# Attention in a two-layer decoder trunk: one matmul for the scores of both kinds of keys, and the compressed branch's products stacked along the contraction

## The chip, the core and the metric

The kernel runs on one core of a Trainium2 chip. The metric is the device time of one execution in microseconds (us). Of the engines, TensorE (PE in the rows; its weight loads are PEld) does the matmuls and transposes, VectorE (DVE) and ScalarE (ACT) do the elementwise work, GpSimd (POOL) small side work, and SyncE (SP) issues the weight transfers.

## The reference, cut to what matters

Two layers; in each, a feed-forward block, a mixer with three branches, and a second feed-forward block, over 256 tokens of width 1024. The change is in the mixer's sparse attention, which has 8 heads of width 64 in 2 groups of 4 heads that share keys and values. For the 256 tokens here it computes, for each head:

```python
# compressed branch: 15 keys, one for each 32 tokens at a stride of 16
s_c = einsum('bqghd,bgnd->bghqn', qp, kc) * scale
p_c = masked_softmax(s_c, cmp_end <= t)
o_c = einsum('bghqn,bgnd->bqghd', p_c, vc)
# selected blocks (all 4 blocks of 64 tokens are taken) and sliding window (512 >= 256 tokens):
# with this length both are plain causal attention, each with keys and values of its own
s_s = einsum('bqghd,bgqld->bghql', qr, ks) * scale ; p_s = masked_softmax(s_s, m_s)
s_w = einsum('bqghd,bkgd->bghqk', qr, kw) * scale  ; p_w = masked_softmax(s_w, m_w)
return g[..., 0:1] * o_c + g[..., 1:2] * o_s + g[..., 2:3] * o_w
```

All of it is float32. The kernel keeps that precision by splitting an operand into a rounded high part and a low rest, and by adding three matmuls (high by high, high by low, low by high).

## The kernel before, in words

The 256 tokens are two tiles of 128 rows, t = 0 and t = 1. Each tile is a stream, written as a Python generator that runs through both layers; the program takes steps of the two streams in turn. A step is the matmuls of one unit of weights: 1024 columns, six matmuls of 512 columns (three for each of two pieces). The weights of a unit come by a transfer on SP's queue, are split into a high and a low part by ScalarE (`whi`, lines 272 and 276) and VectorE (`wlo`, lines 273 and 277) up to 4 steps ahead, and lie in 8 pairs of buffers.

Beside the streams runs a list of background tasks, up to four at a time (`background`, line 1063). After each step of a stream one task gets one turn, and each task names after a turn how many steps it wants to rest: `ATT_A, ATT_B, ATT_C, ATT_D = 1, 3, 2, 3`. Attention is made of such tasks. The stream of a tile waits for their result only ahead of its last branch product (`until ... S["ynsa"][t]`). The final order on each engine's queue is not quite that of the program: it is set when the kernel is built, where an instruction that is expected to be ready may pass an earlier one that is not.

For each tile and layer there are four tasks `nsa_attention(t, l, var, g)` (line 730): `var` is the kind of keys (0 selected, 1 window), `g` the group of heads. A task of the first tile sees 128 keys. It does eight matmuls of 128 columns into one PSUM bank `s` (4 heads, high and low keys, line 745), adds the causal mask, takes the maximum and the exponentials (lines 750 to 757), scales by the reciprocal sum and the gate (line 764), transposes the four blocks of probabilities (line 769), splits them into `ph` and `pl` (lines 368 and 369), and adds three matmuls of 512 columns into the tile's bank `o` (line 788). With the call that ends it, a task of the first tile takes five turns. A task of the second tile sees 256 keys: it works through two banks `s`, each with four matmuls of 256 columns, and two blocks of keys, in seven turns.

The compressed branch has one task `cmp_attention` for each tile and layer (line 895). Its probabilities are 128 tokens by 8 heads by 16 keys, `sc`, 128 columns in all; one transpose (line 918) turns them, a copy and a subtraction split them into `phc`. The values were laid out by `compress` (line 795) as `vbd`, block-diagonal by head: for each of 4 heads in a group a 128 by 128 weight, in a high and a low form (line 890). For each of the four the task does three matmuls of 128 columns, 12 in all (line 788).

PSUM has 8 banks: 6 for accumulators (`acc`, `br`, `s`, `sc`, `o` and others, in turn), 2 for transposes (`pt`). Temporaries of 520 columns have 8 buffers in turn.

Of the kernel before, what the change touches and what calls it, by code (L numbers as in the profile page):

```python
# [21 lines left out]
F32 = mybir.dt.float32  # L22
# [6 lines left out]
P = 128  # L29
# [49 lines left out]
class Nothing:  # L79
    """Stands in for engines, pools and tiles while the order of the weight units is found."""  # L80

# [13 lines left out]
def view(ap, off, dims):  # L95
    if isinstance(ap, Nothing):
        return ap
    return bass.AP(tensor=ap.tensor, offset=ap.offset + off, ap=[list(ap.ap[0])] + [list(d) for d in dims])


def f32(ap):
    return ap.bitcast(F32)
# [18 lines left out]
def program(nc, pools, a, out, plan):  # L121
# [21 lines left out]
    def tbank():  # L143
        return pst.tile([P, 512], F32, name="pt", tag="t")
# [4 lines left out]
    def ttile(name, dt=F32):  # L149
        return tp.tile([P, 520], dt, name=name, tag="tmp")  # L150

# [1 line left out]
    x = [consts.tile([P, D], F32, name=f"x{t}") for t in range(2)]  # L153
# [36 lines left out]

# [1 line left out]
    now = [0]  # L192
# [186 lines left out]

# [1 line left out]
    def rstd(halves):  # L381
# [63 lines left out]

# [1 line left out]
    def ffn(t, l, which):  # L447
# [34 lines left out]

# [1 line left out]
    dmask = consts.tile([P, P], F32, name="dmask")  # L484
    cmadd = consts.tile([P, 2, 16], F32, name="cmadd")
    cm01 = consts.tile([P, 2, 16], F32, name="cm01")
    bmask = consts.tile([P, 8], F32, name="bmask")
    cosT = consts.tile([P, 2, 8], F32, name="cosT")
    sinT = consts.tile([P, 2, 8], F32, name="sinT")
# [3 lines left out]
    def setup():  # L493
# [6 lines left out]
        for t in range(2):  # L500
            for m, fill in ((cmadd, NEG), (cm01, 0.0)):
# [6 lines left out]
        nc.gpsimd.affine_select(bmask, bmask, pattern=[[16, 8]], compare_op=OP.is_ge, fill=0.0,  # L508
                                base=15, channel_multiplier=-1)
        for t in range(2):  # L510
            nc.gpsimd.memset(f32(vz[t]), 0.0)
# [41 lines left out]

# [1 line left out]
    shared = {}  # L555
# [46 lines left out]

# [1 line left out]
    def rope(src, n, t, write):  # L604
# [117 lines left out]
    def recip_gate(sums, n, gate):  # L722
        r = sp.tile([P, n], F32, name=f"rg{n}")
        nc.vector.tensor_scalar(r, sums, 1e-30, None, op0=OP.max)
        nc.vector.reciprocal(r, r)
        if gate is not None:
            nc.vector.tensor_mul(r, r, gate)
        return r

    def nsa_attention(t, l, var, g):  # L730
        S = shared[l]
        QT = S["QT"][t][1]
        KT = [k.rearrange("p (v k) -> p v k", v=4) for k in S["KT"]]
        gt = S["gt"][t]
        nk = t + 1
        hp = 4 // nk
        sums = sp.tile([P, 4], F32, name="sums")
        pu = []
        for u in range(nk):
            s = bank("s")  # L740
            s3 = s.rearrange("p (i k) -> p i k", i=hp)
            for i in range(hp):
                lhsT = QT[:, g * 4 + u * hp + i]
                for j in range(2):
                    nc.tensor.matmul(s3[:, i], lhsT=lhsT, rhs=KT[j][:, var * 2 + g, 0:nk * P],  # L745
                                     start=(i == 0 and j == 0), stop=(i == hp - 1 and j == 1),
                                     skip_group_check=True)
            yield ATT_A
            dg = s3[:, :, t * P:(t + 1) * P]
            nc.vector.tensor_tensor(dg, dg, view(dmask, 0, [[0, hp], [1, P]]), op=OP.add)  # L750
            nm = sp.tile([P, hp], F32, name=f"nm{hp}")
            nc.vector.tensor_reduce(nm, s3, axis=AX.X, op=OP.max, negate=True)
            p = ttile("p")
            p3 = p[:, :512].rearrange("p (i k) -> p i k", i=hp)
            for i in range(hp):
                c = u * hp + i
                nc.scalar.activation(p3[:, i], s3[:, i], AF.Exp, bias=nm[:, i:i + 1], accum_out=sums[:, c:c + 1])
            pu.append(p3)
        yield ATT_B
        r = recip_gate(sums, 4, view(gt, g * 12 + 1 + var, [[3, 4]]))  # L760
        for u in range(nk):
            for i in range(hp):
                c = u * hp + i
                nc.vector.tensor_scalar(pu[u][:, i], pu[u][:, i], r[:, c:c + 1], None, op0=OP.mult)
        yield ATT_C
        for kt in range(nk):
            pt = tbank()
            for c in range(4):
                nc.tensor.transpose(pt[:, c * P:(c + 1) * P], pu[c // hp][:, c % hp, kt * P:(kt + 1) * P], ident)
            ph, pl = ttile("ph", F32R), ttile("pl", F32R)  # L770
            evac_split(ph[:, :512], pl[:, :512], pt)
            yield ATT_D
            vh = vz[kt][:, var * 512 + g * 128:var * 512 + g * 128 + 128]
            vl = vz[kt][:, var * 512 + 256 + g * 128:var * 512 + 256 + g * 128 + 128]
            accumulate(t, l, 1, [(None, st, mv[:, :512]) for st, mv in ((vh, ph), (vh, pl), (vl, ph))], kt == nk - 1)

    def accumulate(t, l, part, products, last):
        S = shared[l]
        first = S["o"][t] is None
        if first:  # L780
            S["o"][t] = bank("o")
        o = S["o"][t]
        if last:
            S["parts"][t] += 1
        closing = last and S["parts"][t] == 5
        for n, (i, st, mv) in enumerate(products):
            dst = o if i is None else o[:, i * P:(i + 1) * P]
            nc.tensor.matmul(dst, lhsT=st, rhs=mv, start=(first and (n == 0)),  # L788
                             stop=(closing and n == len(products) - 1), skip_group_check=True)
        if closing:  # L790
            y = gtile("ynsa", F32R)
            evac_split(y[:, 0:512], y[:, 512:1024], o)
            S["ynsa"][t] = y

    def compress(l, i):
# [68 lines left out]
        else:  # L864
# [4 lines left out]
            gr = ttile("gr", F32R)  # L869
            out_v = gr[:, 0:256].rearrange("p (a i n) -> p a i n", a=4, i=4)  # L870
            out_l = gr[:, 256:512].rearrange("p (a i n) -> p a i n", a=4, i=4)
            src = view(u1, 0, [[16, 4], [0, 4], [1, 16]])
            nc.scalar.copy(out_v, src)
# [3 lines left out]
            for ht in range(2):  # L877
                mm3(ps[:, 0:64], gr[:, ht * P:(ht + 1) * P], gr[:, 256 + ht * P:256 + (ht + 1) * P],
                    wh[:, ht], wl[:, ht], ht == 0, ht == 1)
            vs = sp.tile([P, 64], F32, name="vs")  # L880
            nc.scalar.copy(vs, ps[:, 0:64])
            vbd = gtile("vbd", F32R)
            vf = sp.tile([P, 64], F32R, name="vf")
            nc.scalar.copy(vf, vs)
            vlo = sp.tile([P, 64], F32, name="vlo")
            nc.vector.tensor_sub(vlo, vs, f32(vf))
            msk = view(bmask, 0, [[1, 4], [4, 2], [0, 64]])
            for j, sv in enumerate((f32(vf), vlo)):
                dst = vbd[:, j * 512:(j + 1) * 512].rearrange("p (i g d) -> p i g d", i=4, g=2)
                nc.vector.tensor_tensor(dst, view(sv, 0, [[0, 4], [0, 2], [1, 64]]), msk, op=OP.mult)  # L890
            S["VBD"] = vbd
            for tt in range(2):
                add(("nsa", l, tt), cmp_attention(tt, l))

    def cmp_attention(t, l):
# [18 lines left out]
        r = recip_gate(sm, 8, view(S["gt"][t], 0, [[3, 8]]))  # L914
        nc.vector.tensor_tensor(sc, sc, view(r, 0, [[1, 8], [0, 16]]), op=OP.mult)
        yield ATT_B
        pt = tbank()
        nc.tensor.transpose(pt[:, :P], sc.rearrange("p h n -> p (h n)"), ident)
        ph = ttile("phc", F32R)
        evac_split(ph[:, 0:P], ph[:, P:2 * P], pt[:, :P])  # L920
        yield ATT_D
        vbd = S["VBD"]
        products = []
        for i in range(4):
            vh, vl = vbd[:, i * P:(i + 1) * P], vbd[:, 512 + i * P:512 + (i + 1) * P]
            products += [(i, st, mv) for st, mv in ((vh, ph[:, 0:P]), (vh, ph[:, P:2 * P]), (vl, ph[:, 0:P]))]
        accumulate(t, l, 0, products, True)

# [122 lines left out]

# [1 line left out]
    pending, lanes, counts = [], [], {}  # L1053
# [26 lines left out]
    def mixer(t, l):  # L1080
# [21 lines left out]
        def attend():  # L1102
            for var in range(2):
                for g in range(2):
                    add(("nsa", l, t), nsa_attention(t, l, var, g))

# [109 lines left out]
```

## Time and profile before

| what | value |
|---|---|
| median of 3 timed runs | 1317.28 us (1317.2 to 1317.69) |
| the profiled execution: span from first to last instruction | 1314.1 us |
| its own time, with what lies around the span | not on the page; the median is 3.2 us above the span |
| instructions | 17407 |
| TensorE matmuls | 6266, busy 1300.3 us |
| VectorE, ScalarE, GpSimd busy | 896.6 us, 743.0 us, 76.5 us |
| transfers | 240.76 MB, mean 183 GB/s |
| mean granted TensorE clock | 0.999 |

Matmuls are pipelined: the record of one lasts longer than the time until the next one starts. What a matmul takes from the engine is read from the distance of two starts, not from its own length.

### The profile page before, as it was taken

To read this page: it belongs to the slowest core of one execution; us is meant where nothing else is said; L and a number is where in the kernel's file an instruction comes from. 1 tells how busy PE (TensorE), PEld (TensorE's weight loads), DVE (VectorE), ACT (ScalarE), POOL (GpSimd) and SP (SyncE) were. 2 spreads that over 40 slices of the span, in tenths; PEclk is the share of its full clock that TensorE was granted. 3 is DMA by queue.
4 is the path that set the end of the run, shared out by engine and by line. 5 is a ranking of instruction groups with operands and counts; after the bars stand their busy time and mean duration, and the time that the engine had idled before them with its cause. 6 is when DMAs were issued, how large, how long until landed. Compare 5 with 4: busy or idle time off the path is not lost.

```text
span 1314.1 us, 17407 instructions
## 1 busy us (share of the span) xinstructions
PE 1300.3 (99%) x6266; PEld 1078.9 (82%) x6266; DVE 896.6 (68%) x1363; ACT 743.0 (57%) x1195; POOL 76.5 (6%) x184
## 2 busy tenths in 40 slices
PE   9999999999999999999999999999999999999998
PEld 7888888878888888888888888888888888888886
DVE  6666556989887666565575665579898866766643
ACT  6645546886664465454464555568666554645542
POOL 3010101200000010000010001013000000100000
PEclk9999999999999999999999999999999999999999
DMA  8665575764445655655756665657644456566552
GB/s 273 210 192 181 180 220 175 224 214 144 139 134 159 198 187 180 191 192 180 229 168 191 188 209 177 209 167 230 191 144 145 133 159 210 176 188 189 183 190 80
DMA packets 118950, 240.76 MB, mean 183 GB/s; under 512 B 8176, under 2 KB 26768, under 8 KB 118864
## 3 DMA queue, kind: packets, MB, share of 16 engines
q1 hardware_dynamic: 118256, 239.30, 58.0%
q8 instruction: 49, 0.80, 0.2%
q0 software_dynamic: 576, 0.34, 0.1%
q14 instruction: 37, 0.30, 0.1%
q10 hardware_dynamic: 32, 0.01, 0.0%
HBM read 238.57 MB, written 1.05 MB: 182 GB/s over the span
## 4 chain that ended last, share of the span: by engine, by line
PE 90%; DVE 4%; ACT 2%; DMA 2%; issue 1%; POOL 0%; SPq 0%; DVEq 0%; POOLq 0%; ACTq 0%
PE acc L334 19%; PE acc L336 19%; PE acc L335 19%; PE y L336 7%; PE y L335 7%; PE y L334 7%; PE pt L377 3%; PE o L788 2%; PE br L334 2%; PE br L335 2%; PE br L336 2%; DVE wlo L277 1%; DMA raw<-in_ffn_w_in_dram 1%; PE s L745 1%; ACT whi L276 1%
## 5 line engine op out<-in xcount | busy, mean ns | idle before, releaser
L277 DVE SCALAR_TENSOR_TENSOR wlo<-raw,gT,whi 128x512 fp32r<-128x512 f32 (+2 forms) x432 | 397.6, 938 | 208.0 <-ACT whi L276 206.7
L276 ACT ACTIVATE whi<-raw,gT 128x512 fp32r<-128x512 f32 (+2 forms) x432 | 365.9, 874 | 295.3 <-PE acc L336 216.6
L334 PE MATMUL acc<-whi,hThi 128*128 128x512 f32 (+1 forms) x1184 | 468.6, 396 | 1.0 <-ACT hThi L368 1.0
L336 PE MATMUL acc<-whi,hTlo 128*128 128x512 f32 (+1 forms) x1184 | 459.1, 389 | 0.0
L335 PE MATMUL acc<-wlo,hThi 128*128 128x512 f32 (+1 forms) x1184 | 458.6, 388 | 0.1
L336 PEld LDWEIGHTS acc<-whi,hTlo 128*128 128x128 f32 x1184 | 222.1, 188 | 46.9 <-DVE hTlo L369 0.6
L334 PEld LDWEIGHTS acc<-whi,hThi 128*128 128x128 f32 x1184 | 222.5, 188 | 43.1 <-ACT hThi L368 1.8
L335 PEld LDWEIGHTS acc<-wlo,hThi 128*128 128x128 f32 x1184 | 222.7, 188 | 41.8 <-DVE wlo L277 0.8
L273 DVE TENSOR_TENSOR wlo<-raw,whi 128x1024 fp32r<-128x1024 f32 x144 | 176.0, 1224 | 108.2 <-ACT whi L272 106.1
L272 ACT CAST whi<-raw 128x1024 fp32r<-128x1024 f32 x144 | 151.2, 1051 | 130.9 <-PE acc L336 70.6
L334 PE MATMUL y<-whi,gT 128*128 128x512 f32 x352 | 138.1, 392 | 0.0
L336 PE MATMUL y<-whi,gT 128*128 128x512 f32 x352 | 137.4, 390 | 0.0
L335 PE MATMUL y<-wlo,gT 128*128 128x512 f32 x352 | 137.4, 390 | 0.0
L389 POOL TENSOR_TENSOR nr<-nv,mhalf 128x1 f32<-128x1 f32 x28 | 19.9, 712 | 1017.6 <-DVE nv L387 1013.8
L336 PEld LDWEIGHTS y<-whi,gT 128*128 128x128 f32 x352 | 66.1, 188 | 13.8
L335 PEld LDWEIGHTS y<-wlo,gT 128*128 128x128 f32 x352 | 66.1, 188 | 13.3
L334 PEld LDWEIGHTS y<-whi,gT 128*128 128x128 f32 x352 | 66.1, 188 | 13.3
L368 ACT CAST gT<-pt 128x512 fp32r<-128x512 f32 (+1 forms) x48 | 26.1, 543 | 23.3 <-PE pt L377 23.3
L456 DVE SCALAR_TENSOR_TENSOR th<-th,rs,acc 128x512 f32<-128x512 f32 (+1 forms) x48 | 33.7, 703 | 4.5
L454 ACT ACTIVATE th<-acc,rs 128x512 f32<-128x512 f32 (+1 forms) x48 | 31.0, 646 | 7.6 <-PE acc L336 5.8
L455 DVE SCALAR_TENSOR_TENSOR th<-th,acc 128x512 f32<-128x512 f32 (+1 forms) x48 | 30.7, 640 | 6.2 <-ACT th L454 4.4
L369 DVE TENSOR_TENSOR gT<-pt,gT 128x512 fp32r<-128x512 f32 (+1 forms) x48 | 30.9, 643 | 3.9 <-ACT gT L368 3.4
(284 smaller groups left out, 1229.4 us busy)
## 6 DMA issues: line engine op xcount, KB each, us to landing
raw<-in_ffn_w_in_dram SPq DMA_DIRECT2D x160, 512.0 KB, 4.0
raw<-in_w_mix_in_dram SPq DMA_DIRECT2D x96, 512.0 KB, 4.1
raw<-in_ffn_w_out_dram SPq DMA_DIRECT2D x88, 512.0 KB, 3.5
raw<-in_ffn_w_in_dram SPq DMA_DIRECT2D x32, 256.0 KB, 2.9
raw<-in_w_mem_kv_dram SPq DMA_DIRECT2D x16, 512.0 KB, 4.6
raw<-in_w_mix_out_dram SPq DMA_DIRECT2D x16, 512.0 KB, 3.7
gB<-in_ffn_norm_post_dram SPq DMA_DIRECT2D x8, 512.0 KB, 5.6
raw<-in_cmp_k_w_dram SPq DMA_DIRECT2D x8, 512.0 KB, 4.0
```

Of the source, the lines that this page charges most:

```text
L272: nc.scalar.copy(h, v)
L273: nc.vector.tensor_sub(w, v, f32(h))
L276: nc.scalar.activation(h, v, AF.Copy, scale=g)
L277: nc.vector.scalar_tensor_tensor(w, v, g, f32(h), op0=OP.mult, op1=OP.subtract)
L334: nc.tensor.matmul(ps, lhsT=xh, rhs=wh, start=start, stop=False, skip_group_check=skip)
L335: nc.tensor.matmul(ps, lhsT=xh, rhs=wl, start=False, stop=False, skip_group_check=skip)
L336: nc.tensor.matmul(ps, lhsT=xl, rhs=wh, start=False, stop=stop, skip_group_check=skip)
L369: nc.vector.tensor_sub(lo, ps, f32(hi))
L377: nc.tensor.transpose(pt[:, j * P:(j + 1) * P], src[:, c0 + j * P:c0 + (j + 1) * P], ident)
L454: nc.scalar.activation(th[:, :n], pa[:, :n], AF.Tanh, scale=r_half)
L455: nc.vector.scalar_tensor_tensor(th[:, :n], th[:, :n], 1.0, pa[:, :n], op0=OP.add, op1=OP.mult)
L456: nc.vector.scalar_tensor_tensor(th[:, :n], th[:, :n], r2_half, pb[:, :n], op0=OP.mult, op1=OP.mult)
```

## The change

For the first tile, `nsa_attention` becomes `nsa_first(l, g)`: one task for both kinds of keys. A matmul takes as its moving operand the selected and the window keys of the group side by side (two pieces of 128 columns, 512 apart in `KT`), so each has 256 columns and there are half as many. A task holds two banks `s` one after the other (two heads each), has the softmax of 4 blocks for each, one reciprocal over 8 sums, and then for each kind of keys the four transposes, the split and the three products as before. It takes seven turns; there are two such tasks for each layer in place of four. For the second tile, `nsa_second` is what `nsa_attention` was.

In the compressed branch the probabilities are laid out for each of 4 head pairs as 96 columns: 32 (two heads of 16 keys), and the same 32 twice more (one copy by ScalarE). Four transposes of 96 columns put them side by side into one bank, 96 rows by 512 columns. One copy rounds all 96 rows; one subtraction puts the low rest into rows 32 to 63. The values are one weight `vst` of 96 rows: high, high, low. One matmul with a contraction of 96 rows and 512 columns then does what the 12 did. `compress` makes 96 columns in place of 128 for the product `vc`, and `vst` (64 by 128 and 32 by 128) in place of `vbd` (two of 128 by 512). A mask `gmask` is made once, by one reduction on VectorE. The order of adding the tasks changes from kind by group to group.

The diff, cut to its core (lines of `nsa_attention` that only move are left out, and removed comments):

```diff
@@ setup @@
+        nc.vector.tensor_reduce(gmask, view(bmask, 0, [[1, 2], [2, 4]]), axis=AX.X, op=OP.add)
@@ attention @@
+    def values(t, var, g):
+        c = var * 512 + g * 128
+        return vz[t][:, c:c + 128], vz[t][:, c + 256:c + 384]
+
+    def softmax_part(s3, dg, sums, c0, p3):
+        n = s3.shape[1] if not dry else 1
+        nc.vector.tensor_tensor(dg, dg, view(dmask, 0, [[0, n], [1, P]]), op=OP.add)
+        nm = sp.tile([P, n], F32, name=f"nm{n}")
+        nc.vector.tensor_reduce(nm, s3, axis=AX.X, op=OP.max, negate=True)
+        for i in range(n):
+            nc.scalar.activation(p3[:, i], s3[:, i], AF.Exp, bias=nm[:, i:i + 1], accum_out=sums[:, c0 + i:c0 + i + 1])
+
+    def turn_probabilities(parts):
+        pt = tbank()
+        for c, part in enumerate(parts):
+            nc.tensor.transpose(pt[:, c * P:(c + 1) * P], part, ident)
+        ph, pl = ttile("ph", F32R), ttile("pl", F32R)
+        evac_split(ph[:, :512], pl[:, :512], pt)
+        return ph, pl
+
+    def weighted_values(t, l, kt, var, g, ph, pl, last):
+        vh, vl = values(kt, var, g)
+        accumulate(t, l, 1, [(st, mv[:, :512]) for st, mv in ((vh, ph), (vh, pl), (vl, ph))], last)
+
+    def nsa_first(l, g):
+        S = shared[l]
+        QT = S["QT"][0][1]
+        sums = sp.tile([P, 8], F32, name="sums")
+        pu = []
+        for u in range(2):
+            s = bank("s")
+            s2 = s.rearrange("p (i c) -> p i c", i=2)
+            for i in range(2):
+                for j in range(2):
+                    nc.tensor.matmul(s2[:, i], lhsT=QT[:, g * 4 + u * 2 + i],
+                                     rhs=view(S["KT"][j], g * 256, [[512, 2], [1, P]]),
+                                     start=(i == 0 and j == 0), stop=(i == 1 and j == 1), skip_group_check=True)
+            yield ATT_A
+            s4 = s.rearrange("p (c k) -> p c k", c=4)
+            p = ttile("p")
+            p4 = p[:, :512].rearrange("p (c k) -> p c k", c=4)
+            softmax_part(s4, s4, sums, u * 4, p4)
+            pu.append(p4)
+        yield ATT_B
+        r = recip_gate(sums, 8, view(S["gt"][0], g * 12 + 1, [[3, 4], [1, 2]]))
+        for u in range(2):
+            for c in range(4):
+                nc.vector.tensor_scalar(pu[u][:, c], pu[u][:, c], r[:, u * 4 + c:u * 4 + c + 1], None, op0=OP.mult)
+        yield ATT_C
+        for var in range(2):
+            ph, pl = turn_probabilities([pu[h // 2][:, h % 2 * 2 + var] for h in range(4)])
+            yield ATT_D
+            weighted_values(0, l, 0, var, g, ph, pl, True)
...
@@ compress @@
-            src = view(u1, 0, [[16, 4], [0, 4], [1, 16]])
+            src = view(u1, 0, [[32, 2], [0, 3], [1, 32]])
...
-                mm3(ps[:, 0:64], gr[:, ht * P:(ht + 1) * P], gr[:, 256 + ht * P:256 + (ht + 1) * P],
+                mm3(ps[0:96, 0:64], gr[:, ht * 96:(ht + 1) * 96], gr[:, 192 + ht * 96:192 + (ht + 1) * 96],
                     wh[:, ht], wl[:, ht], ht == 0, ht == 1)
...
-            for j, sv in enumerate((f32(vf), vlo)):
-                dst = vbd[:, j * 512:(j + 1) * 512].rearrange("p (i g d) -> p i g d", i=4, g=2)
-                nc.vector.tensor_tensor(dst, view(sv, 0, [[0, 4], [0, 2], [1, 64]]), msk, op=OP.mult)
+            vst = sp.tile([P, 128], F32R, name="vst", bufs=1)
+            for p0, p1, sv in ((0, 64, f32(vf)), (64, 96, vlo)):
+                nc.vector.tensor_tensor(vst[p0:p1].rearrange("p (g d) -> p g d", g=2),
+                                        view(sv[p0:p1], 0, [[0, 2], [1, 64]]),
+                                        view(gmask[p0:p1], 0, [[1, 2], [0, 64]]), op=OP.mult)
@@ cmp_attention @@
-        nc.vector.tensor_tensor(sc, sc, view(r, 0, [[1, 8], [0, 16]]), op=OP.mult)
+        pc = ttile("pc")
+        nc.vector.tensor_tensor(view(pc, 0, [[96, 4], [16, 2], [1, 16]]), view(sc, 0, [[16, 4], [64, 2], [1, 16]]),
+                                view(r, 0, [[1, 4], [4, 2], [0, 16]]), op=OP.mult)
+        nc.scalar.copy(view(pc, 32, [[96, 4], [32, 2], [1, 32]]), view(pc, 0, [[96, 4], [0, 2], [1, 32]]))
         yield ATT_B
         pt = tbank()
-        nc.tensor.transpose(pt[:, :P], sc.rearrange("p h n -> p (h n)"), ident)
+        for i in range(4):
+            nc.tensor.transpose(pt[0:96, i * P:(i + 1) * P], pc[:, i * 96:(i + 1) * 96], ident)
         ph = ttile("phc", F32R)
-        evac_split(ph[:, 0:P], ph[:, P:2 * P], pt[:, :P])
+        nc.scalar.copy(ph[0:96, :512], pt[0:96])
+        nc.vector.tensor_sub(ph[32:64, :512], pt[32:64], f32(ph[32:64, :512]))
         yield ATT_D
...
+        accumulate(t, l, 0, [(S["VST"][0:96], ph[0:96, :512])], True)
@@ mixer, attend @@
-            for var in range(2):
-                for g in range(2):
-                    add(("nsa", l, t), nsa_attention(t, l, var, g))
+            for g in range(2):
+                if t == 0:
+                    add(("nsa", l, t), nsa_first(l, g))
+                else:
+                    for var in range(2):
+                        add(("nsa", l, t), nsa_second(l, var, g))
```

## Rows read from the trace of the kernel before

**Rows 1.** The page: busy us (share of span) x instructions; then the chain.

```profile
PE 1300.3 (99%) x6266; PEld 1078.9 (82%) x6266; DVE 896.6 (68%) x1363; ACT 743.0 (57%) x1195; POOL 76.5 (6%) x184
...
PE 90%; DVE 4%; ACT 2%; DMA 2%; issue 1%; POOL 0%; SPq 0%; DVEq 0%; POOLq 0%; ACTq 0%
```

**Rows 2.** Windows, attention of layer 0: length, PE, PEld, DVE, ACT busy, clock, DMA.

```profile
300.00:340.00 40.00, 40.00 (x216) 34.02 (x215) 36.20 (x91) 26.23 (x64) 0.88 (x3) 1.00 0.44 133
340.00:440.00 100.00, 100.00 (x501) 83.87 (x500) 74.97 (x142) 56.60 (x105) 0.00 (x0) 1.00 0.52 154
```

**Rows 3.** Line 745, one of its two rows: count, ns min/median/max, first and last, forms.

```profile
L745 PE MATMUL s<-KTh,QT x64: 220/277/283, 283.1 to 1034.9; 128*128 128x128 f32 x32, 128*128 128x256 f32 x32
```

**Rows 4.** Timeline: start us, length us, operation. First tile's scores, eight matmuls.

```profile
297.05 0.22 PE L745 MATMUL s<-KTh,QT 128*128 128x128 f32 x1
...
298.18 0.39 PE L335 MATMUL acc<-wlo,hThi 128*128 128x512 f32 x1
```

**Rows 5.** Timeline, second tile's scores: two blocks of four matmuls.

```profile
355.92 0.28 PE L745 MATMUL s<-KTh,QT 128*128 128x256 f32 x1
...
357.78 0.28 PE L745 MATMUL s<-KTh,QT 128*128 128x256 f32 x1
...
358.49 0.40 PE L335 MATMUL acc<-wlo,hThi 128*128 128x512 f32 x1
```

**Rows 6.** Timeline, the compressed branch's 12 products.

```profile
1057.50 1.45 PE L788 MATMUL o<-phc,vbd 128*128 128x128 f32 x12
...
1059.07 0.39 PE L335 MATMUL acc<-wlo,hThi 128*128 128x512 f32 x1
```

**Rows 7.** Timeline, two products of 512 columns into the same bank.

```profile
352.71 0.39 PE L788 MATMUL o<-pl,vz 128*128 128x512 f32 x1
352.94 0.39 PE L788 MATMUL o<-ph,vz 128*128 128x512 f32 x1
```

**Rows 8.** Timeline, four transposes and one, each with the second matmul behind it.

```profile
1049.38 0.60 PE L769 MATMUL pt<-ident,p 128*128 128x128 f32 x4
...
1050.05 0.39 PE L335 MATMUL br<-wlo,ymemh 128*128 128x512 f32 x1
...
1051.20 0.27 PE L918 MATMUL pt<-ident,sc 128*128 128x128 f32 x1
...
1051.54 0.39 PE L335 MATMUL acc<-wlo,hThi 128*128 128x512 f32 x1
```

**Rows 9.** Timeline: eight matmuls with 64 and 32 weight columns by turns, then transposes.

```profile
254.32 0.28 PE L821 MATMUL z<-whi,FHL 128*64 128x256 f32 x1
254.44 0.28 PE L823 MATMUL z<-wlo,FHL 128*32 128x256 f32 x1
...
255.26 0.81 PE L708 MATMUL pt<-ident_r,qe 128*128 128x128 f32 x8
255.90 0.46 PE L334 MATMUL acc<-whi,hThi 128*128 128x512 f32 x1
```

**Rows 10.** Timeline, PE's wait behind the first block of scores, layer 0.

```profile
286.74 0.66 PE L377 MATMUL pt<-ident,qms 128*128 128x128 f32 x4 [0.77 <-ACT qms L932]
```

**Rows 11.** Timeline, a bank of scores: first matmul, last exponential read from it.

```profile
288.17 0.22 PE L745 MATMUL s<-KTh,QT 128*128 128x128 f32 x1
...
292.54 0.38 ACT L757 ACTIVATE p<-s,nm 128x128 f32<-128x128 f32 x1
```

**Rows 12.** Tile phc: the split of the compressed probabilities, 128 columns, ns.

```profile
L368 ACT CAST phc<-pt x4: 246/256/267, 402.1 to 1065.9; 128x128 fp32r<-128x128 f32 x4
L369 DVE TENSOR_TENSOR phc<-pt,phc x4: 281/284/293, 402.5 to 1066.7; 128x128 fp32r<-128x128 f32 x4
```

**Rows 13.** Tile o: the same two operations over 512 columns, ns.

```profile
L368 ACT CAST ynsa<-o x4: 586/587/589, 409.7 to 1070.7; 128x512 fp32r<-128x512 f32 x4
L369 DVE TENSOR_TENSOR ynsa<-o,ynsa x4: 684/688/692, 411.4 to 1071.4; 128x512 fp32r<-128x512 f32 x4
```

More of the change, by code (lines that the diff above doesn't have):

```diff
@@ L487, in program @@
     bmask = consts.tile([P, 8], F32, name="bmask")
+    gmask = consts.tile([P, 2], F32, name="gmask")
     cosT = consts.tile([P, 2, 8], F32, name="cosT")
@@ L728, in recip_gate @@
         return r
-    def nsa_attention(t, l, var, g):
-        S = shared[l]
-        QT = S["QT"][t][1]
+    def values(t, var, g):
[8 more added lines that the diff above has]
+            nc.scalar.activation(p3[:, i], s3[:, i], AF.Exp, bias=nm[:, i:i + 1], accum_out=sums[:, c0 + i:c0 + i + 1])
@@ L733, in nsa_attention, with nsa_second @@
+    def nsa_second(l, var, g):
+        S = shared[l]
+        QT = S["QT"][1][1]
         KT = [k.rearrange("p (v k) -> p v k", v=4) for k in S["KT"]]
-        gt = S["gt"][t]
-        nk = t + 1
-        hp = 4 // nk
         sums = sp.tile([P, 4], F32, name="sums")
         pu = []
-        for u in range(nk):
+        for u in range(2):
             s = bank("s")
-            s3 = s.rearrange("p (i k) -> p i k", i=hp)
-            for i in range(hp):
-                lhsT = QT[:, g * 4 + u * hp + i]
+            s3 = s.rearrange("p (i k) -> p i k", i=2)
+            for i in range(2):
@@ L744, in nsa_attention @@
                 for j in range(2):
-                    nc.tensor.matmul(s3[:, i], lhsT=lhsT, rhs=KT[j][:, var * 2 + g, 0:nk * P],
-                                     start=(i == 0 and j == 0), stop=(i == hp - 1 and j == 1),
-                                     skip_group_check=True)
+                    nc.tensor.matmul(s3[:, i], lhsT=QT[:, g * 4 + u * 2 + i], rhs=KT[j][:, var * 2 + g],
+                                     start=(i == 0 and j == 0), stop=(i == 1 and j == 1), skip_group_check=True)
@@ L748, in nsa_attention @@
             yield ATT_A
[L749 to L752, printed above, removed]
             p = ttile("p")
[L754 to L757, printed above, removed]
+            p3 = p[:, :512].rearrange("p (i k) -> p i k", i=2)
@@ L758, in nsa_attention @@
+            softmax_part(s3, s3[:, :, P:2 * P], sums, u * 2, p3)
             pu.append(p3)
         yield ATT_B
[L760 to L764, printed above, removed]
-        yield ATT_C
[L766 to L771, printed above, removed]
+        r = recip_gate(sums, 4, view(S["gt"][1], g * 12 + 1 + var, [[3, 4]]))
@@ L772, in nsa_attention @@
+        for h in range(4):
+            part = pu[h // 2][:, h % 2]
+            nc.vector.tensor_scalar(part, part, r[:, h:h + 1], None, op0=OP.mult)
+        yield ATT_C
+        for kt in range(2):
+            ph, pl = turn_probabilities([pu[h // 2][:, h % 2, kt * P:(kt + 1) * P] for h in range(4)])
             yield ATT_D
-            vh = vz[kt][:, var * 512 + g * 128:var * 512 + g * 128 + 128]
-            vl = vz[kt][:, var * 512 + 256 + g * 128:var * 512 + 256 + g * 128 + 128]
-            accumulate(t, l, 1, [(None, st, mv[:, :512]) for st, mv in ((vh, ph), (vh, pl), (vl, ph))], kt == nk - 1)
+            weighted_values(1, l, kt, var, g, ph, pl, kt == 1)
@@ L785, in accumulate @@
         closing = last and S["parts"][t] == 5
-        for n, (i, st, mv) in enumerate(products):
-            dst = o if i is None else o[:, i * P:(i + 1) * P]
-            nc.tensor.matmul(dst, lhsT=st, rhs=mv, start=(first and (n == 0)),
+        for n, (st, mv) in enumerate(products):
+            nc.tensor.matmul(o, lhsT=st, rhs=mv, start=(first and (n == 0)),
                              stop=(closing and n == len(products) - 1), skip_group_check=True)
@@ L869, in compress @@
             gr = ttile("gr", F32R)
-            out_v = gr[:, 0:256].rearrange("p (a i n) -> p a i n", a=4, i=4)
-            out_l = gr[:, 256:512].rearrange("p (a i n) -> p a i n", a=4, i=4)
-            src = view(u1, 0, [[16, 4], [0, 4], [1, 16]])
+            out_v = gr[:, 0:192].rearrange("p (a r n) -> p a r n", a=2, r=3)
+            out_l = gr[:, 192:384].rearrange("p (a r n) -> p a r n", a=2, r=3)
+            src = view(u1, 0, [[32, 2], [0, 3], [1, 32]])
             nc.scalar.copy(out_v, src)
@@ L877, in compress @@
             for ht in range(2):
-                mm3(ps[:, 0:64], gr[:, ht * P:(ht + 1) * P], gr[:, 256 + ht * P:256 + (ht + 1) * P],
+                mm3(ps[0:96, 0:64], gr[:, ht * 96:(ht + 1) * 96], gr[:, 192 + ht * 96:192 + (ht + 1) * 96],
                     wh[:, ht], wl[:, ht], ht == 0, ht == 1)
             vs = sp.tile([P, 64], F32, name="vs")
-            nc.scalar.copy(vs, ps[:, 0:64])
-            vbd = gtile("vbd", F32R)
+            nc.scalar.copy(vs[0:96], ps[0:96, 0:64])
             vf = sp.tile([P, 64], F32R, name="vf")
-            nc.scalar.copy(vf, vs)
+            nc.scalar.copy(vf[0:96], vs[0:96])
             vlo = sp.tile([P, 64], F32, name="vlo")
-            nc.vector.tensor_sub(vlo, vs, f32(vf))
-            msk = view(bmask, 0, [[1, 4], [4, 2], [0, 64]])
-            for j, sv in enumerate((f32(vf), vlo)):
-                dst = vbd[:, j * 512:(j + 1) * 512].rearrange("p (i g d) -> p i g d", i=4, g=2)
-                nc.vector.tensor_tensor(dst, view(sv, 0, [[0, 4], [0, 2], [1, 64]]), msk, op=OP.mult)
-            S["VBD"] = vbd
+            nc.vector.tensor_sub(vlo[64:96], vs[64:96], f32(vf[64:96]))
+            vst = sp.tile([P, 128], F32R, name="vst", bufs=1)
[3 more added lines that the diff above has]
+                                        view(gmask[p0:p1], 0, [[1, 2], [0, 64]]), op=OP.mult)
+            S["VST"] = vst
             for tt in range(2):
@@ L914, in cmp_attention @@
         r = recip_gate(sm, 8, view(S["gt"][t], 0, [[3, 8]]))
-        nc.vector.tensor_tensor(sc, sc, view(r, 0, [[1, 8], [0, 16]]), op=OP.mult)
+        pc = ttile("pc")
+        nc.vector.tensor_tensor(view(pc, 0, [[96, 4], [16, 2], [1, 16]]), view(sc, 0, [[16, 4], [64, 2], [1, 16]]),
+                                view(r, 0, [[1, 4], [4, 2], [0, 16]]), op=OP.mult)
+        nc.scalar.copy(view(pc, 32, [[96, 4], [32, 2], [1, 32]]), view(pc, 0, [[96, 4], [0, 2], [1, 32]]))
         yield ATT_B
         pt = tbank()
-        nc.tensor.transpose(pt[:, :P], sc.rearrange("p h n -> p (h n)"), ident)
+        for i in range(4):
+            nc.tensor.transpose(pt[0:96, i * P:(i + 1) * P], pc[:, i * 96:(i + 1) * 96], ident)
         ph = ttile("phc", F32R)
-        evac_split(ph[:, 0:P], ph[:, P:2 * P], pt[:, :P])
+        nc.scalar.copy(ph[0:96, :512], pt[0:96])
+        nc.vector.tensor_sub(ph[32:64, :512], pt[32:64], f32(ph[32:64, :512]))
         yield ATT_D
[L922 to L927, printed above, removed]
+        accumulate(t, l, 0, [(S["VST"][0:96], ph[0:96, :512])], True)
     def mem_query(t, l, ps, r):
```

## The prediction

> **What bounds the kernel now.** I read the page's first part first. TensorE is busy 1300.3 us of a span of 1314.1 us; VectorE has 68% and ScalarE 57% [rows 1]. That leaves TensorE 13.8 us without a matmul in flight, about 1% of the span. The chain of waits agrees: 90% of what ends last is TensorE's own work [rows 1]. Then the windows over the attention of layer 0, the stretch that the change edits: TensorE is busy 40.00 of 40 us and then 100.00 of 100 us [rows 2]. So a matmul removed there is time removed, unless another engine takes TensorE's place; the nearest is VectorE, busy 36.20 us of the first 40 [rows 2]. Transfers take a share of 0.44 to 0.52 there and the granted clock is 1.00, the 2.4 GHz level [rows 2]; neither is a limit.
>
> The lengths of matmuls overstate them. Two products of 512 columns start 0.23 us apart though each lasts 0.39 us [rows 7]. I therefore price a block of matmuls by the distance from its first start to the start of the second ordinary 512-column matmul behind it, less one ordinary distance of 0.23 us; the first matmul behind a block of short ones starts early, which this takes in.
>
> **Scores of the first tile.** Before, 4 tasks for each layer do 8 matmuls of 128 columns: 8 blocks in two layers, 64 matmuls, as the row with 32 of that form says for one of the two key parts [rows 3]. A block runs from 297.05 to 298.18: 1.13 - 0.23 = 0.90 us [rows 4]. After, there are also 8 blocks, each of four matmuls of 256 columns. The second tile does exactly that form already: 357.78 to 358.49, 0.71 - 0.23 = 0.48 us [rows 5]. A matmul of 256 columns thus costs 0.48 / 4 = 0.12 us and one of 128 columns 0.90 / 8 = 0.11: the same for twice the columns. Saved: 8 x 0.42 = 3.4 us. The moving operand is now two pieces 512 columns apart, which no row shows with 256 columns; I give it nothing. Were it to cost, it could be no more than the old block, so this term lies between 0 and 3.4.
>
> **Products of the compressed branch.** Twelve matmuls take 1059.07 - 1057.50 - 0.23 = 1.34 us [rows 6]; there are four such blocks (two tiles, two layers). After, one matmul of 512 columns, 0.23 us by the same form with 128 rows [rows 7]. Saved: 4 x 1.11 = 4.4 us. A contraction of 96 rows is not in the trace: at worst the matmul shows its whole length, 0.39 us, which takes back 4 x 0.16 = 0.6 us; I see no way for it to be below 0.23, since the 512 columns remain.
>
> **Transposes of the compressed branch.** One becomes four. Four cost 0.67 - 0.23 = 0.44 us, one 0.34 - 0.23 = 0.11 us [rows 8]. Added: 4 x 0.33 = 1.3 us. Their weights have 96 columns in place of 128. The cheapest transposes of the trace take 0.64 / 8 = 0.08 us each [rows 9], which would make it 4 x 0.24 = 1.0; a transpose that overlaps nothing lasts 0.27 us [rows 8] and would make it 4 x (4 x 0.27 - 0.11) = 3.9. I take the 1.3, the nearest form. In the Trainium skill, TensorE: Matmul & The Clock Gate (LDWEIGHTS) has the load time go with the weight's columns, 96 / 1.2 = 80 ns as an estimate of mine; by that the term would be 1.0 as well. No run here shows a load of 96 columns.
>
> **The rest on TensorE.** `compress` keeps its 6 matmuls of 64 columns for each layer, with weights of 96 columns. By the bounds just used each changes by between 0 and -0.03 us, at most 0.4 us over 12; I take 0. The second tile's tasks and the three products for each kind of keys stay as they are.
>
> **ScalarE and VectorE.** For each of the four compressed tasks, ScalarE's rounding grows from 128 columns (0.26 us, [rows 12]) to 512 (0.59 us, [rows 13]) and one copy of 128 columns (0.26) is added: +0.59 us. VectorE's subtraction goes from 0.28 to 0.69 us [rows 12, 13]: +0.4 us, two for each layer. Against it VectorE loses two multiplications of 512 columns for `vbd` (0.69 each by the same width), gets two small ones (0.28 each by [rows 12]), and half of the small reciprocal operations, so its sum is about even or lower. I cost all this at nothing on the path: the task rests 3 steps after each of these places, and a step is 6 x 0.23 = 1.4 us, so 4.1 us cover a chain that is about 1 us longer. If that cover were gone, the tile's result would come 1 us later, and only the last branch product waits for it, with a task list that now ends 6 turns of a layer earlier (20 turns of the first tile's tasks become 14). The one reduction for `gmask` in the setup is a small VectorE operation, up to 0.3 us by the nearest row [rows 12], in the first microseconds or beside feed-forward work; nothing. No transfer is added, removed or moved; SP's and POOL's queues keep their order.
>
> **A wait that may take part of it.** Right behind the first block of scores TensorE waits for ScalarE's `qms`, 0.77 us without a matmul in flight [rows 10], once in each layer. `qms` doesn't come sooner because the block is 0.42 us shorter. If the queue keeps its order, the wait grows by 0.42 and that block's gain is gone: 0.8 us in two layers. The transposes stand there because the order made at build put them amid a step's matmuls; with a shorter block more matmuls may be put ahead of them, and nothing is lost. I take half, 0.4 us.
>
> **Sum.** -3.4 - 4.4 + 1.3 + 0.4 = -6.1 us on the span of 1314.1, which makes 1308.0. What lies around the span isn't touched; the median is 3.2 us above the span, and 1317.28 - 6.1 = 1311.2 us.
>
> **Rivals.**
>
> *VectorE becomes the bound where the first tile attends.* The same masks, maxima, scalings and splits now fall into 14 turns in place of 20, so for those turns this work is 1.4 times as dense, where VectorE has 3.8 us of 40 free [rows 2]. Were VectorE to set the pace there, the score blocks' 3.4 us would not be had: 1314.6. Against it: weights are split up to 4 steps ahead, 5.5 us of cover, and VectorE also loses the wide multiplications in this stretch.
>
> *The 96-row forms don't overlap with their neighbours.* Each change of form would then cost the overlapped part of a matmul, 0.39 - 0.23 = 0.16 us [rows 7]: into and out of the transposes and the product (16 changes), and of the `vc` block (4), 20 x 0.16 = 3.2 us, which makes 1314.4. Against it: matmuls with 64 and with 32 weight columns alternate at (255.26 - 254.32) / 8 = 0.12 us each and pay nothing of the kind [rows 9]. The Trainium skill, TensorEngine Tiling (Array Packing), Key Properties, says that changing the tiling mode drains TensorE. By that rule these alternating forms should pay; as far as columns go the trace does not agree, and for rows no run here shows it.
>
> *A bank that isn't free: slower.* A task of the first tile now asks for its second bank one turn after the first, while the first is still being read. A bank is held for 292.54 + 0.38 - 288.17 = 4.75 us [rows 11]; a turn is a step and a block, 1.4 + 0.5 = 1.9 us. If all six accumulator banks were taken, the second block's matmuls would stand on TensorE's queue, and all behind them, for 4.75 - 1.9 = 2.9 us; four tasks make 11.4 us, and 1322.6. It decides from two of the four tasks on (5.7 of the 6.1 us gone) and is slower than before by more than the measurement's grain from three. Against it: the second tile's tasks ask in this same way, with two blocks 1.86 us apart [rows 5], in a stretch in which TensorE has no gap in 100 us [rows 2].
>
> *Better than the sum.* The reordered queue also covers the waits for `qms`, which are in the 13.8 us: 0.8 us for each of two, and the 0.4 I took off: about 1309.
>
> **How the numbers follow.** Forecast 1311.2: 0.66, with its own range of 1309.5 to 1313. VectorE 0.14, the 96-row forms 0.08, the bank 0.05, better 0.07. A difference under 0.2% (2.6 us, so above 1314.6) can't be told from no change. The two rivals at 1314.4 and 1314.6 stand on that line, and I count about half of each as faster: 0.66 + 0.07 + 0.06 + 0.04 = 0.83 faster; slower 0.06, the bank and a remainder; within 0.2% the other 0.11. The range reaches from the better case to just past the two middle rivals, 1309.2 to 1315.0, and so takes in the unknown prices above except the transposes at their full length.
>
> **What would show it.** In the changed kernel: score blocks of the first tile with four matmuls of 256 columns at 0.12 us; one `o` product at 0.23 us in place of 12; four transposes at 0.11; TensorE's time without a matmul still near 13 us; the wait for `qms` between 0.8 and 1.2 us. VectorE as the bound would show as waits of TensorE for `wlo` or `nm` between the first scores and about 60 us later. The bank would show as a gap ahead of a first tile's second block of scores. The prediction is wrong if TensorE's busy time falls by 6 us and its idle time rises by more than 2, or if short forms with 96 rows stand further apart than 0.11 (transposes) or 0.23 us (product).

## The result and the profile after

The changed kernel took 1308.91 us (median of 4 runs, 1308.7 to 1309.18), the kernel before 1317.24 us in the same comparison (4 runs, 1315.89 to 1317.69): a ratio of 0.9939, 95% interval 0.9925 to 0.9953. Run twice more on other occasions it gave 0.9938 (0.9925 to 0.9952) and 0.9931 (0.9918 to 0.9943). So it is faster, by 8 to 9 us.

The page of the changed kernel, its first part and the chain, answers to [rows 1]:

```profile
PE 1294.7 (99%) x6202; PEld 1072.7 (82%) x6202; DVE 893.5 (68%) x1352; ACT 744.5 (57%) x1199; POOL 75.3 (6%) x184
...
PE 89%; DVE 5%; ACT 2%; DMA 2%; issue 1%; POOL 0%; DVEq 0%; POOLq 0%; ACTq 0%
```

TensorE is still the bound: 64 matmuls fewer (32 scores fewer, 44 products fewer, 12 transposes more) and 5.6 us less busy. The span of the profiled execution is 1307.2 us, 6.9 below that of before. The windows of the attention in layer 0 answer to [rows 2]:

```profile
300.00:340.00 40.00, 39.91 (x210) 33.21 (x209) 36.55 (x93) 25.05 (x54) 0.49 (x3) 1.00 0.54 162
340.00:440.00 100.00, 100.00 (x492) 83.62 (x491) 75.33 (x138) 57.63 (x104) 0.00 (x0) 1.00 0.55 158
```

VectorE is a little denser in the first 40 us (36.55 in place of 36.20), and TensorE still has no gap that counts.

Now the blocks, each in the timeline of the changed kernel (start us, length us, operation). The first tile's scores, which answer to [rows 4]; then the one product, to [rows 6]; then the four transposes, to the single one in [rows 8]:

```profile
284.01 0.28 PE L766 MATMUL s<-KTh,QT 128*128 128x256 f32 x1
...
284.72 0.40 PE L335 MATMUL acc<-wlo,hThi 128*128 128x512 f32 x1
...
391.96 0.60 PE L959 MATMUL pt<-ident,pc 128*96 128x128 f32 x4
...
392.63 0.39 PE L335 MATMUL br<-wlo,ymemh 128*128 128x512 f32 x1
...
398.60 0.40 PE L825 MATMUL o<-phc,vst 96*128 96x512 f32 x1
...
399.07 0.40 PE L335 MATMUL acc<-wlo,hThi 128*128 128x512 f32 x1
```

A score block is 284.72 - 284.01 - 0.23 = 0.48 us, the product 399.07 - 398.60 - 0.23 = 0.24, the transposes 392.63 - 391.96 - 0.23 = 0.44. The columns side by side don't cost more than the contiguous ones of [rows 5]; 96 rows cost no more than 128.

The `vc` block in `compress`, two neighbours in the changed kernel and then two in the kernel before:

```profile
289.74 0.25 PE L336 MATMUL vc<-w2vh,gr 128*96 128x64 f32 x1
289.82 0.25 PE L334 MATMUL vc<-w2vh,gr 128*96 128x64 f32 x1
```

```profile
290.59 0.28 PE L336 MATMUL vc<-w2vh,gr 128*128 128x64 f32 x1
290.70 0.28 PE L334 MATMUL vc<-w2vh,gr 128*128 128x64 f32 x1
```

With 96 weight columns they start 0.08 us apart, with 128 columns 0.11: 12 of them make about 0.3 us.

What the engines waited for, TensorE's rows (us in all, times, longest), first before and then after:

```profile
PE pt L377 <- ACT qms L932: 1.6, 2, 0.8
...
PE pt L831 <- ACT zc L827: 1.2, 2, 0.7
...
PE pt L377 <- DVE th L456: 0.4, 1, 0.4
```

```profile
PE pt L868 <- ACT zc L864: 1.5, 2, 0.7
...
PE pt L377 <- DVE th L456: 0.8, 1, 0.8
```

The wait for `qms`, once in each layer, is gone. The place in the changed kernel, which answers to [rows 10]:

```profile
285.87 0.28 PE L766 MATMUL s<-KTh,QT 128*128 128x256 f32 x1
...
287.04 0.40 PE L334 MATMUL acc<-whi,hThi 128*128 128x512 f32 x1
287.30 0.66 PE L377 MATMUL pt<-ident,qms 128*128 128x128 f32 x4
```

Before, the transposes of `qms` started 1.16 us after the matmul ahead of them in layer 0 (285.58 to 286.74) and 1.20 in layer 1; now 0.26 and 0.27. Two things made up the 0.9 us, about half each.

*The place of the transposes came later.* Between the first block of scores and them there stood 8 matmuls of 512 columns; now there stand 10, and the second block of scores. Counted from the first score matmul, the last matmul ahead of them started after 2.53 us before (283.05 to 285.58) and starts after 3.03 us now (284.01 to 287.04): 0.50 us later, 0.54 in layer 1.

*`qms` came sooner.* ScalarE starts it 2.96 us after the first score matmul before (286.01) and 2.55 now (286.56): 0.41 us sooner, 0.39 in layer 1. It stands there behind the copy `gr`, which needs the last step of a tile `u` from VectorE. Before, VectorE waited 0.75 us and then did two splits `wlo` ahead of that step. Now the shorter block of scores is ready while VectorE stands idle, the causal mask goes first, and one `wlo` stands behind the step. TensorE, VectorE and ScalarE in the kernel before:

```profile
283.05 0.22 PE L745 MATMUL s<-KTh,QT 128*128 128x128 f32 x1
...
285.58 0.39 PE L335 MATMUL acc<-wlo,hThi 128*128 128x512 f32 x1
```

```profile
284.01 0.75 DVE L277 SCALAR_TENSOR_TENSOR wlo<-raw,gT,whi 128x512 fp32r<-128x512 f32 x1 [0.75 <-ACT whi L276]
...
284.78 0.75 DVE L277 SCALAR_TENSOR_TENSOR wlo<-raw,gT,whi 128x512 fp32r<-128x512 f32 x1
285.44 0.22 DVE L844 TENSOR_TENSOR u<-u,zs 128x64 f32<-128x64 f32 x1
```

```profile
285.69 0.41 ACT L873 CAST gr<-u 128x256 fp32r<-128x256 f32 x1 [0.96 <-DVE u L844]
286.01 0.68 ACT L932 ACTIVATE qms<-acc,rs 128x512 f32<-128x512 f32 x1
```

VectorE and ScalarE in the changed kernel:

```profile
284.69 0.70 DVE L738 TENSOR_TENSOR s<-s,dmask 128x512 f32<-128x512 f32 x1 [0.46 <-PE s L766]
...
285.39 0.74 DVE L277 SCALAR_TENSOR_TENSOR wlo<-raw,gT,whi 128x512 fp32r<-128x512 f32 x1
286.06 0.22 DVE L881 TENSOR_TENSOR u<-u,zs 128x64 f32<-128x64 f32 x1
```

```profile
286.31 0.35 ACT L910 CAST gr<-u 128x192 fp32r<-128x192 f32 x1 [0.61 <-DVE u L881]
286.56 0.68 ACT L969 ACTIVATE qms<-acc,rs 128x512 f32<-128x512 f32 x1
```

**The account of the span.** Scores 8 x (0.90 - 0.48) = -3.4; products 4 x (1.34 - 0.24) = -4.4; transposes 4 x (0.44 - 0.11) = +1.3; `vc` -0.3: -6.8 us by blocks. The waits for `qms` -1.8. The distance ahead of `zc` +0.3. And the profiled execution of the changed kernel stood 0.8 us later at 219 us, long before any edited matmul. The sum is -7.5, against 6.9 us of the spans; the remaining 0.6 is spread over edges of blocks and isn't told apart. The medians differ by 1.4 us more than the spans. That is the choice of the execution: a run's time lies some 1.7 us above its span (1308.89 and 1307.2 for the profiled execution of the changed kernel, 1315.79 and 1314.1 for a run of the kernel before), so the profiled execution before took about 1315.8 us, 1.4 less than the median. It was one of the fastest; the 3.2 us that were taken as lying around the span hold this 1.4 too. The forecast doesn't change by it.

### The profile page after: what moved, and what is told of

It is laid out like the page before. It is cut to its first block, busy times and chain, and to the rows that moved or that the text cites. A ratio compares the mean times of both kernels' runs of the same rounds, so it can differ in the third digit from the quotient of the medians.

```text
span 1307.2 us, 17269 instructions
## 1 busy us (share of the span) xinstructions
PE 1294.7 (99%) x6202; PEld 1072.7 (82%) x6202; DVE 893.5 (68%) x1352; ACT 744.5 (57%) x1199; POOL 75.3 (6%) x184
## 4 chain that ended last, share of the span: by engine, by line
PE 89%; DVE 5%; ACT 2%; DMA 2%; issue 1%; POOL 0%; DVEq 0%; POOLq 0%; ACTq 0%
PE acc L334 18%; PE acc L336 18%; PE acc L335 18%; PE y L336 7%; PE y L335 7%; PE y L334 7%; PE pt L377 3%; DVE wlo L277 2%; PE br L334 2%; PE br L335 2%; PE br L336 2%; PE o L825 1%; DMA raw<-in_ffn_w_in_dram 1%; ACT whi L276 1%; DVE wlo L273 1%
```

## The experiments

Two theories. D: the time follows the distance of starts on TensorE, and the wait for `qms` goes as well. Q: it is the order on the queues, from 14 turns in place of 20, and the number of matmuls is by the way.

**e0_after.** The changed kernel, as the base for the next three.

> The changed kernel again, as the base for the others on the same chip. Theory D (the gain is start distance on TensorE, 6.7 us by the blocks, plus 1.8 us of waits for qms that went): about 7 to 8 us below the kernel before, ratio 0.994 to 0.995. Theory Q (the gain is a luckier order on the queues, from 14 turns in place of 20, and not the number of matmuls): the same here; it differs in the next three.

Measured: 1309.0 us, before 1317.08 (18 runs), ratio 0.9938 (0.9925 to 0.9952), 8.1 us less.

**e1_scores.** The scores part alone:

```diff
+    nsa_first, nsa_second, softmax_part, ... as in the changed kernel
     compress, cmp_attention, accumulate as before (vbd, one transpose, 12 products)
```

> Only the scores part: two tasks for the first tile with matmuls of 256 columns; the compressed branch as before (one transpose, 12 products). Theory D: 8 score blocks save 0.42 us each, 3.4 us, and the waits for qms go as in the changed kernel, 1.8 us: 5.2 us below before, ratio 0.9960. Theory Q: nearly the whole gain is here, 7 us or more, ratio 0.9945 or below.

Measured: 1312.26 us, ratio 0.9965 (0.9953 to 0.9978), 4.8 us less. Its trace has no wait of TensorE's matmuls for `qms` (0.31 and 0.32 us of distance). D's 5.2 fits; Q's 7 doesn't: the interval ends at 0.9953, above its 0.9945.

**e2_products.** The compressed branch alone:

```diff
     nsa_attention as before, four tasks
+    compress, cmp_attention as in the changed kernel (vst, four transposes, one product)
```

> Only the compressed branch's part: four transposes of 96 columns, one product; the first tile's scores in four tasks of 128 columns as before. Theory D: products -4.4, transposes +1.3, the vc block -0.3: 3.4 us below before, ratio 0.9974, and the wait for qms stays at about 0.8 us in each layer. Theory Q: no gain, since turns and order stay: within 1 us of before.

Measured: 1313.53 us, ratio 0.9973 (0.9963 to 0.9983), 3.6 us less. D said 3.4. The wait for `qms` stands as before, as its row among TensorE's waits says:

```profile
PE pt L377 <- ACT qms L934: 1.5, 2, 0.8
```

The two parts add up: 4.8 + 3.6 = 8.4, against 8.1 for both. Q falls as the account of the whole gain: this part has the old turns and has its gain.

**e3_narrow.** Only the width taken back:

```diff
-                    nc.tensor.matmul(s2[:, i], lhsT=..., rhs=view(S["KT"][j], g * 256, [[512, 2], [1, P]]), ...)
+                    for v in range(2):
+                        nc.tensor.matmul(s2[:, i, v * P:(v + 1) * P], lhsT=..., rhs=view(S["KT"][j], v * 512 + g * 256, [[1, P]]), ...)
```

> The changed kernel with each score matmul of 256 columns of the first tile made as two of 128 columns again (8 matmuls a block, 8 blocks); tasks, turns and all else as changed. Theory D: 8 x 0.42 = 3.4 us above the changed kernel, 4 to 5 us below before, ratio 0.9965; no wait for qms above 0.3 us. Theory Q: as the changed kernel, within 1 us.

Measured: 1314.63 us, ratio 0.9982 (0.9973 to 0.9991): 5.6 us above the changed kernel, where D had 3.4. The score blocks are back at 0.90 us, as it should be. The rest are waits in its trace that the changed kernel doesn't have; the first one, and two of TensorE's rows of waits:

```profile
287.72 0.27 PE L767 MATMUL s<-KTl,QT 128*128 128x128 f32 x1
288.34 0.66 PE L377 MATMUL pt<-ident,qms 128*128 128x128 f32 x4 [0.34 <-ACT qms L971]
```

```profile
PE pt L377 <- DVE v L1044: 1.1, 3, 0.7
...
PE pt L377 <- ACT qms L971: 0.7, 2, 0.4
```

D's expectation of a `qms` distance under 0.3 us was wrong here (0.61 and 0.65). The place of the transposes has not moved: they now stand right behind the second block, and the matmul ahead of them starts 3.02 us after the first score matmul (284.70 to 287.72), where the changed kernel has 3.03. But `qms` starts 2.90 us after it and not 2.55, with the `gr` ahead of it behind two `wlo` of VectorE again:

```profile
284.70 0.22 PE L767 MATMUL s<-KTh,QT 128*128 128x128 f32 x1
```

```profile
287.60 0.68 ACT L971 ACTIVATE qms<-acc,rs 128x512 f32<-128x512 f32 x1
```

So of the 0.9 us of this wait in each layer, 0.35 hangs on the width, by way of VectorE's order, and 0.5 on the turns, where Q was right about a part. The other 0.05 is the narrower `gr`: in e2, which has it without the rest, `qms` starts at 2.90 us in place of 2.96. The transposes of `v` wait for VectorE. Width is worth 3.4 us in the blocks; the 2.2 us above that, waits that came with the new order, were not taken apart one by one.

**e4_later_qms.** The kernel before, and one number:

```diff
-        later(2, turn)      # mem_query
+        later(3, turn)
```

> The kernel before, with one edit: the transposes of qms come one step of a stream later (3 in place of 2). Theory D says that the waits for qms are worth 1.8 us by themselves: about 1.8 us below before, ratio 0.9986, TensorE's waits for qms under 0.3 us in each layer. If the wait only moves to the next thing that ScalarE is late with: ratio 1.000.

Measured: 1315.6 us against 1317.43, ratio 0.9989 (0.998 to 0.9998), 1.8 us less. In its trace the transposes follow the scores at the usual distance:

```profile
288.60 0.28 PE L745 MATMUL s<-KTl,QT 128*128 128x128 f32 x1
288.71 0.62 PE L377 MATMUL pt<-ident,qms 128*128 128x128 f32 x4
```

That prices the wait by itself at 1.8 us, with an interval of 0.3 to 2.6, and the distances in the trace say the same (0.9 us in each layer). Without it the change would have given about 8.1 - 1.8 = 6.3 us; this is worked out from e0 and e4, not run.

**e5_later_zc and e6_both.** The waits that are left, taken one by one from the changed kernel:

```diff
         nc.scalar.copy(zc[0:64, 0:256], z[0:64, 0:256])
-        yield 1
+        yield 2                                   # e5 and e6
...
         nc.vector.tensor_sub(Fr[:, :, 1], Fv, f32(Fr[:, :, 0]))
-        yield 2
+        yield 3                                   # e6; and gmask by two additions on GpSimd
```

> The changed kernel, with the transposes of zc in the compression one turn later (2 in place of 1). The distance ahead of them was 1.1 to 1.7 us in each layer, 0.23 without a wait: 1.8 to 2.9 us below the changed kernel if the wait goes and the order behind it holds; no gain or a loss of up to 2 us if the turn's shift makes the wait for qms come back.

> As the last one, and the products z one turn later behind FHL (3 in place of 2; 0.45 us in each layer), and gmask by two small additions on GpSimd in place of the reduction on VectorE. 2.7 to 4.5 us below the changed kernel if all three waits go, ratio to before 0.991; otherwise as the last one.

Measured: 1310.49 us, ratio 0.9948 (0.9935 to 0.996), and 1310.94 us, ratio 0.9952 (0.9939 to 0.9964); before 1317.43. Neither gains. The waits that were aimed at are gone from both traces, and others stand there, of the transposes of `qe`, first in e5 and then in e6:

```profile
PE pt L710 <- DVE zs L874: 2.1, 2, 1.0
...
PE pt L710 <- DVE qe L701: 1.0, 2, 0.7
```

```profile
PE pt L712 <- DVE qe L703: 3.6, 2, 1.8
```

**e7_gmask_pool.** The changed kernel with `gmask` on GpSimd:

```diff
-        nc.vector.tensor_reduce(gmask, view(bmask, 0, [[1, 2], [2, 4]]), axis=AX.X, op=OP.add)
+        nc.gpsimd.tensor_tensor(bsum, bmask[:, 0:4], bmask[:, 4:8], op=OP.add)
+        nc.gpsimd.tensor_tensor(gmask, bsum[:, 0:2], bsum[:, 2:4], op=OP.add)
```

> The changed kernel, with gmask by two small additions on GpSimd. Where gmask is reduced on VectorE the ffn's first output block began 0.7 to 1.3 us later in the traces than without it. If the reduction is the cause: TensorE reaches the first wait behind y at about 218.5 us of the span (219.3 now), and 0.7 us below the changed kernel, too little for the times to tell. If that is chance of the start: still 219 us or later.

Measured: 1309.54 us, ratio 0.9942 (0.9929 to 0.9954). TensorE reached the mark at 219.6 us, so with the reduction taken off VectorE the start is no earlier. Most of what differs lies in the first 10 us: the first matmul of the feed-forward block started at 8.07 us before, at 8.71 in the changed kernel and at 8.86 here. Its wait for `hThi` goes from 0.4 to 2.0 us over the runs and isn't longest where the start is latest. `gmask` itself isn't cleared by this: the ten profiled executions that make `gmask`, on either engine, reached the mark at 219.1 to 219.8 us, the three that don't (before, e1, e4) at 218.5 to 218.9. Whether that is `gmask` or chance, no run shows.

**e8_both_qe and e9_zc_qe.** The same two with the transposes of `qe` one step later as well:

```diff
-        later(2, turn(0))
-        later(4, turn(1))
+        later(3, turn(0))
+        later(5, turn(1))
```

> The kernel with the three later steps (zc, FHL, gmask on GpSimd), and the transposes of qe one step later as well (3 and 5 in place of 2 and 4): there the wait had moved, 2.05 and 2.11 us of distance where 0.12 is usual. If it now goes: 3.8 us below that kernel, about 1307, ratio to before 0.9923, below the changed kernel by 1.5 us or more. If a wait only moves on to the next late operand: no better than the changed kernel, 0.994 or more.

> The changed kernel with only zc one turn later and the transposes of qe one step later. In the kernel with zc alone the distances ahead of qe were 1.41 in layer 0, and 0.89 and 1.44 in layer 1, 0.12 usual, 3.4 us too much: if they go, 3 us below that kernel, about 1307.5, ratio to before 0.993. If a wait moves on: as the changed kernel or above it.

**e10_after.** The changed kernel beside them.

> The changed kernel once more, as the base for the two others on this chip: ratio to before 0.994.

Measured: 1308.82 us (0.993, 0.9918 to 0.9943), 1308.95 us (0.9931, 0.9917 to 0.9944), and the changed kernel 1308.63 us (0.9931, 0.9918 to 0.9943). By the medians they win back the 2 us that e5 and e6 had lost, and no more; the intervals overlap, so the times alone don't show even that. In e9 the transposes of `qe` still wait, 1.5 us in all where e5 had 3.1. In e8 the waits have moved on again, to the copy behind the transposes that were moved:

```profile
PE pt L712 <- ACT QT L715: 1.6, 2, 0.9
```

No version among these beats the changed kernel.

## Why the prediction was right, and where it was off

The prediction gave 1311.2 us, 6.1 less than before; 1308.91 was measured, 8.3 less than before, and 0.3 below the low end of the range as written. By the ratio it is 0.9939 x 1317.28 = 1309.2, the low end itself. The blocks were priced right; that the sum missed by 2.2 us comes from one wait with the wrong sign and from a small term at 0. With what the traces show the sum is -3.4 - 4.4 + 1.3 - 0.3 - 1.8 = -8.6 us, against 8.3, 8.1 and 8.8 in the three comparisons.

- *TensorE bounds, so matmul time removed is time removed.* Held: e1 and e2 gained what their blocks and waits say, and no other engine took over.
- *Scores -3.4, products -4.4, transposes +1.3.* Each within 0.1 us of the blocks measured after. The second tile's blocks of [rows 5] were a good price for the first tile's. The lower bound of 1.0 for the transposes was mis-added: four at 0.08 us, less the one at 0.11 that goes, are 0.21 for each block, 0.8 in all. It played no part in the forecast.
- *`vc` at 0.* It gave 0.3 us, within the bound of 0.4. The Trainium skill, TensorE: Matmul & The Clock Gate (LDWEIGHTS), has a load's time go with its columns, 80 ns for 96 as an estimate: the 0.08 us of `vc` agree. The transposes with 96 columns don't: they stayed at 0.11 us each, the price of 128, so their distance doesn't go with the weight's columns; what sets it, no run here shows.
- *ScalarE and VectorE hidden.* Held, though one size was off. The row of the tile `pc`, and then two of the tile `phc`, in the changed kernel (ns min/median/max), which answer to [rows 12]:

```profile
L955 ACT COPY pc<-pc x4: 405/406/406, 389.5 to 1047.6; 128x256 f32<-128x256 f32 x4
```

```profile
L961 ACT CAST phc<-pt x4: 577/580/583, 392.6 to 1051.8; 96x512 fp32r<-96x512 f32 x4
L962 DVE TENSOR_TENSOR phc<-pt,phc x4: 683/684/684, 393.2 to 1053.2; 32x512 fp32r<-32x512 f32 x4
```

  The added copy writes 256 columns, not 128: two repeats of 32 columns for each of 4 pairs. It takes 0.41 us and not 0.26. A subtraction on 32 rows takes as long as one on 128 [rows 13], as assumed.
- *The wait for `qms`, +0.4.* This step failed, with the wrong sign: the wait did not grow by up to 0.42 us in each layer, it went, 1.8 us in two layers. Two of its grounds were off. The prediction named one mechanism (the order made at build may put more matmuls ahead) and weighed it only as something that keeps a loss away. It overlooked that a task of the first tile now issues its second block of scores a turn after its first, so that 0.48 us of scores stand there too: the place came 0.5 us later. And it held that `qms` doesn't come sooner because the block is shorter. It came 0.4 us sooner, through the order on VectorE, and e3, with the width alone taken back, has it 0.35 us later again. e4 shows that the wait is worth 1.8 us; e1 has it gone and e2 has it still, so it goes with the scores part. The case "better than the sum", given 7 in 100, is what happened, nearly half of it by a way that the prediction had ruled out.
- *The rivals.* VectorE as the bound: its busy time in the first 40 us rose by 0.35 us, and between 283 and 440 us TensorE comes late for it once, at 317 us, where the load for the transposes of `v` waits 0.5 us and the matmuls start about 0.25 us late. The 96-row forms: product and transposes stand at 0.24 and 0.11 us, no 0.16 us for each change of form. The bank: the second block starts 1.86 us after the first (284.01, 285.87), with matmuls back to back.

## What to carry to other kernels

Where one engine is busy 99% of the span, price an edit by the distance of starts of the same form elsewhere in the trace, edges included; that came within 0.1 us for scores, products and transposes here. Short matmuls (128 columns and less at 0.11 us each) are the place to look: 12 products of 1.34 us became one of 0.24 us, for three more transposes of 0.33 us together. What such a sum can't give is the few waits that sit where an operand is just late: the order made at build moves them with every edit, they were worth from some 2 us lost (e3, 5.6 measured less 3.4 of width) to 1.8 us gained (e4) in the runs here, and chasing three of them by hand in the changed kernel gained nothing. Such a wait has two ends, the place where the operand is needed and the time at which it comes, and the change moved both: a second block of scores came to stand ahead of the place, and the shorter block let VectorE take its work in another order, which made the operand ready sooner.

## What was not expected

That a wait removed comes back at the next late operand, twice in a row (from `zc` to `qe`, then to `QT`), though TensorE is idle only about 1% of the span. Such a wait can also go by itself: the distance ahead of `zc` was 1.1 to 1.7 us in both layers of two profiled executions of the changed kernel, and 1.43 and 0.35 in the third. And the opening differs from execution to execution: TensorE's wait for the first `hThi` was 0.4 us in one profiled execution of the changed kernel and 1.1 and 1.0 in the two others.
